# A hybrid HGRN2 and retention layer: rotation tables requested one product earlier, gate weights loaded four side steps ahead of their use

## The chip, the cores and the metric

The kernel runs on one NeuronCore of a Trainium2 chip. The metric is the device time of one execution in microseconds (us), the median of several executions. The engines are called as in the profile: PE (TensorE, matmuls), DVE (VectorE), ACT (ScalarE), POOL (GpSimd) and SP (SyncE, which here only issues DMAs). Each engine runs its own queue in order; DMAs are issued from the queues of SP, ACT and POOL.

## What is computed

The layer has one batch, 2048 positions and width 1024, all in float32. In the reference's own lines, cut to what matters here:

```
h = rms_norm(x, norm_g) * (1.0 + scale) + shift     # shift, scale, gate = silu(c) @ w_ada + b_ada
hq, hf, hi, hz, rq, rk, rv, rz, ga, gb = split(h @ w_in)
uA = head_rms_norm(hgrn2(hq, hf, hi), hg_norm_g) * silu(hz)
uB = head_rms_norm(retention(rotary(rq), rotary(rk), rv), ret_norm_g) * silu(rz)
x = x + gate * ((sigmoid(ga) * uA + sigmoid(gb) * uB) @ w_out)
out = rms_norm(x, final_g)
rotary: t1 * cos - t2 * sin, t1 * sin + t2 * cos    # the two halves of a head, by position
```

Two small pieces of it are touched by the change: the cosine and sine tables of the rotation, and the row `gate`, a product of silu(c) with a third of w_ada.

## The kernel before

**Halves and quads.** The positions are worked on in two halves of 1024. Each half runs the same list of 36 "quads" (ORDER, line 44): `a` makes query and forget gate of an HGRN2 head, `v` the values of one HGRN2 and one retention head, `b` query and key of a pair of retention heads, `A` and `B` the output gates of a head. So `b2` is the third retention pair; around it stand `v4 b2 a4 A2 B2 v5 a5 A3 B3 v6 b3 a6`.

**Products.** A quad is 256 columns of the projection for 1024 positions, made by seven products (a Strassen-like scheme, numbered 1 to 7, `product_order`, line 55). A product is 12 matmuls of 128x128 by 128x512, since each float32 operand is split into two fp32r parts. The products of neighbouring quads interleave: for quad n and the quad i ahead of it the order is (2,n), (7,i), (1,n), (5,n), (4,i), (3,n), (6,n). After products 1, 6, 7 and 4 of a quad, one quarter of its result is handed on (`deliver`): product 1 gives columns 0 of position block 0, 6 columns 1 of block 0, 7 columns 1 of block 1, 4 columns 0 of block 1.

**Background.** Beside the products runs other work, written as Python generators: `lanes` (HGRN2 outputs), `rets` (retention), `trees` (the decay tree of an HGRN2 head), and `side`, the work of the change. `bg.tick` is called four times in a product; each fourth tick advances `side` by one `yield`, so a `yield` stands for one product. `posts` are DMA stores that wait a number of ticks.

**Who orders the queues.** PE's instructions are kept in the order of the program. For the other engines the compiler places instructions by priority, which is the order of the program unless a block raises it, and by when their inputs and their buffer are expected to be ready. On the chip a queue then waits in order.

**Shared buffers.** Short-lived tiles of 512 columns come from one pool with six buffers, tag "tp" (`tmp`, NTP = 6): transposed values `vt`, sigmoids `sg` and `sz`, the tables `ct` and `sn`, the swapped half `sw` of the rotation, and the tiles of the side work. A tile that gets a buffer waits for the last reader of the tile before it, a DMA store included. Tag "mu" has four buffers, for the head outputs `mu` that are fetched back for the gating and for the accumulator `acc` of the side work. The PSUM tag "lv" has one bank: the levels of the trees use it, and the small matmuls of the side work too.

**Rotation tables** (`load_rot`, line 685). For each b quad and each of its two position blocks of 512, POOL issues one DMA of 256 KB for the cosines (`ct`, line 689) and two of 128 KB for the signed sines (`sn`, line 691). `take_b` (line 696) reads them: lines 702 and 703 make `sw`, 704 and 705 the result, on DVE, after products 1 and 6 with block 0's tables, after 7 and 4 with block 1's. The calls stand in the main loop: block 0 before product 2 of the b quad, block 1 before its product 6.

**Gate weights** (`ada_row`, line 1334). `gate` is made in two rows of 512 columns. For each of 8 tiles of weights (256 KB) SP issues a load `wg` (line 1338), and DVE adds the tile, scaled, to `acc` (lines 1342, 1344). After the eighth a bias `bg` is loaded, five steps pass, a matmul with a matrix of ones broadcasts the row over the partitions, DVE adds the bias (line 1351), and the row is stored. The rows start in the second half at product 1 of quad v4, one behind the other. Their result is read at the last quad (`load_wo`). In the first half other side work, `next_h` (line 1105), which prepares the second half's inputs, runs from v4 on and holds "tp" buffers too.

**POOL's other work** is small: the reciprocal root of the head norms (lines 186 to 189), on whose result ACT's scaling (line 897) waits, and which is queued with the table loads.

Of the kernel before, what the change touches and what calls it, by code (L numbers as in the profile page):

```python
# [46 lines left out]
def all_quads():  # L47
    return [(sb, x[0], int(x[1])) for sb in range(NSB) for x in ORDER.split()]


QUADS = all_quads()
NQ = len(QUADS)
# [11 lines left out]
def tile_hybrid(ctx: ExitStack, tc: tile.TileContext, a: dict, out: bass.AP):  # L64
# [35 lines left out]
    def bank(name, tag):  # L100
        return pp.tile([P, 512], F32, name=name, tag=tag, bufs=small[tag])

    def tmp(name, cols=512):
        return upool.tile([P, cols], F32, name=name, tag="tp", bufs=NTP)
# [466 lines left out]
    def product(i):  # L571
        m, q = seq[i]
        if m == 2:
            ps = yb[q] = bank(f"y{q}", xtag(q))
        elif m == 1:
            ps = xb[q] = bank(f"x{q}", xtag(q))
        elif m == 5:
            ps = vb[q] = bank(f"v{q}", "v")
        elif m == 3:
            ps = vb[q]  # L580
        else:
            ps = xb[q]
        W.pump(i + NBW)
        for j in range(4):
            if m == 6 and j == 2 and QUADS[q][1] in "AB":
                turned_u(QUADS[q][2], "AB".index(QUADS[q][1]), 0, "v")
            product_step(ps, m, q, j, m in (1, 2, 5) and j == 0, j == 3)
            bg.tick(1.0)
        W.parts.pop((m, q))
        after(m, q)  # L590
# [94 lines left out]
    def load_rot(q, tb):  # L685
        b = QUADS[q][0] * NBLK + tb
        ct, sn = tmp(f"ct{q}_{tb}"), tmp(f"sn{q}_{tb}")
        sl = slice(b * BLK, (b + 1) * BLK)
        G.dma_start(out=ct, in_=lin[0, :, sl].unsqueeze(0).broadcast_to([4, 32, BLK]))
        for two in range(2):  # L690
            G.dma_start(
                out=sn[64 * two : 64 * two + 64, :], in_=lin[1 + two, :, sl].unsqueeze(0).broadcast_to([2, 32, BLK])
            )
        rots[tb] = ct, sn
# [22 lines left out]
    def fetch_u(q, tb):  # L717
        sb, kind, h = QUADS[q]
        s, b = "AB".index(kind), sb * NBLK + tb
        n = 0  # L720
        while usent.get((s, h, b), bg.now) > bg.now - 5.0:
            bg.force()
            n += 1
            if n > 400:
                raise RuntimeError(f"no u {s} {h} {b}")
        if n:
            print("forced u", s, h, b, n)
        ut = mus[h, s, tb] = upool.tile([P, 512], F32, name=f"mu{s}_{h}_{b}", tag="mu", bufs=4)
        nc.sync.dma_start(out=ut, in_=ud[s, h, b])
# [443 lines left out]
    def change_h(sb):  # L1173
        for nm in ("A12", "S1", "A11", "S4", "S2", "S3", "A22"):
            for j in range(4):
                t = combos[sb, nm, j] = a_tile(f"{nm}_{sb}_{j}")
                nc.sync.dma_start(out=t[1].bitcast(F32), in_=hsd[sb, nm, j])
                split_here(t)
                yield
# [154 lines left out]
    def ada_row(j):  # L1334
        acc = upool.tile([P, 512], F32, name=f"acc{j}", tag="mu", bufs=4)
        for kt in range(KT):
            w = tmp(f"wg{j}_{kt}")
            nc.sync.dma_start(out=w, in_=a["w_gate"][j, kt])
            yield
            yield  # L1340
            if kt == 0:
                V.tensor_scalar(out=acc, in0=w, scalar1=sc[:, 0:1], scalar2=None, op0=ALU.mult)
            else:
                V.scalar_tensor_tensor(out=acc, in0=w, scalar=sc[:, kt : kt + 1], in1=acc, op0=ALU.mult, op1=ALU.add)
        bgt = tmp(f"bg{j}")
        nc.sync.dma_start(out=bgt, in_=a["bgate"][:, j * 512 : (j + 1) * 512].broadcast_to([P, 512]))
        for _ in range(5):
            yield
        ps = bank(f"gps{j}", "lv")
        PE.matmul(out=ps, lhsT=ones, rhs=acc, start=True, stop=True)  # L1350
        V.tensor_tensor(out=acc, in0=ps, in1=bgt, op=ALU.add)
        nc.sync.dma_start(out=gated[j], in_=acc)

    def load_wo():
        take("f", 1)
        both = upool.tile([P, 1024], F32, name="gates", tag="f", bufs=1)
        for nh in range(2):
            gate[nh] = both[:, nh * 512 : (nh + 1) * 512]
            nc.sync.dma_start(out=gate[nh], in_=gated[nh])
            for kt in range(KT):  # L1360
                t = wod[kt, nh] = a_tile(f"wo{kt}_{nh}")
                w = tmp(f"wr{kt}_{nh}")
                nc.sync.dma_start(out=w, in_=a["w_o"][kt // 2, nh][:, kt % 2, :])
                V.tensor_tensor(out=w, in0=w, in1=gate[nh], op=ALU.mult)
                split_into(t, w)
                yield

    def out_m(t):
        mts[t] = []
        for q4 in range(2):  # L1370
            m = a_tile(f"m{t}_{q4}")
            nc.sync.dma_start(
                out=m[1].bitcast(F32).rearrange("p (k t) -> p k t", t=P),
                in_=mT_dram[t // 4][4 * q4 : 4 * q4 + 4, :, (t % 4) * P : (t % 4 + 1) * P].rearrange("k p t -> p k t"),
            )
            split_here(m)
            mts[t].append(m)
# [42 lines left out]
    def meet_last():  # L1420
        tag, h, s, tb, fn = waits.pop(0)
        turned_u(h, s, tb, tag)
        fn()

    def some(gen, n):
        for _ in range(n):
            next(gen, None)
# [3 lines left out]
    for i in range(2, len(seq)):  # L1431
        m, q = seq[i]
        kind = QUADS[q][1]
        if m == 6 and 0 in waits:
            meet_last()
        if kind in "AB" and m in (2, 1):
            fetch_u(q, 2 - m)
        if kind == "b" and m == 2:
            load_rot(q, 0)
        if m == 2:  # L1440
            bg.gap = GAP_OF.get(QUADS[q][1:], bg.gap)
        if kind == "b" and m == 6:
            load_rot(q, 1)
        if QUADS[q] == (0, "v", 4) and m == 1:
            bg.side.append(next_h(1))
        if QUADS[q] == (1, "v", 4) and m == 1:
            bg.side.append(chain(ada_row(0), ada_row(1)))
        if (m, q) == (1, mid):
            pro["h"] = change_h(1)
        if (m, q - mid) in NEXT:  # L1450
            some(pro["h"], NEXT[m, q - mid])
        if q == NQ - 1:
            if m == 1:
                pro["w"] = load_wo()
            if m in (6, 7):
                out_m(m - 6)
            if m in (1, 3, 6, 7):
                some(pro["w"], 4)
            if m == 4:
                pro["fg"] = apool.tile([P, 1024], F32, name="fg", tag="A", bufs=NA)  # L1460
                nc.sync.dma_start(out=pro["fg"], in_=a["fg"].broadcast_to([P, 1024]))
                V.tensor_scalar(
                    out=pro["fg"], in0=pro["fg"], scalar1=float(D) ** 0.5, scalar2=None, op0=ALU.mult
                )
        product(i)
# [114 lines left out]
```

## Time and profile before

| | us |
|---|---|
| median of 3 runs | 2015.28 (2014.65 to 2016.09) |
| the profiled execution, its time | 2013.95 |
| its span, first to last instruction | 2012.2 |
| PE busy in the span | 1929.4 (96%) |
| DVE busy | 1419.7 (71%) |
| ACT busy | 984.5 (49%) |
| POOL busy | 300.6 (15%) |
| mean granted clock of PE | 0.988 |

A timeline row gives start, duration, engine (a "q" behind it: its queue issues a DMA), line, operation, output<-inputs, shapes and count; in brackets stands how long the engine was idle before, and what ended that. A waits row gives engine and line, what it waited for, total us, times, longest. In a windows row follow the stretch, its length, and for PE, PEld (weight loads), DVE, ACT and POOL the busy us and number of instructions, then the granted clock, the DMA share and GB/s. A chain row gives start, us and what the chain passed through.

### The profile page before, as it was taken

Reading aid. Unit: us, or ns where it says so; the run is one execution under the profiler, and the core shown is the slowest. Engines: PE = TensorE matmul, PEld = TensorE weight load, DVE = VectorE, ACT = ScalarE, POOL = GpSimd, SP = SyncE. Lnnn points to the kernel's source line nnn. Section 1 sums busy time; section 2 is a strip of 40 time slices with the busy share of each in tenths; the row PEclk is TensorE's granted clock in tenths of the full one; section 3 lists DMA queues with packets and bytes.
Section 4 is the critical chain, followed back from the end, with each engine's and each line's share of the span. In section 5 each row is a group of like instructions: output and inputs, shape, how many; then the busy total and the mean of one; then the engine's idle time right before and its main releaser. Section 6 shows DMA issues by size and latency. Waiting matters only on the chain.

```text
span 2012.2 us, 40017 instructions
## 1 busy us (share of the span) xinstructions
PE 1929.4 (96%) x15172; PEld 1581.1 (79%) x15172; DVE 1419.7 (71%) x2677; ACT 984.5 (49%) x2426; POOL 300.6 (15%) x522
## 2 busy tenths in 40 slices
PE   4899899998999999999999999999999999999998
PEld 3678688887788878887787788878788888887887
DVE  5896767676767777778977676777767775878332
ACT  4635444554456446546444545544454446454331
POOL 3102110221013211201003110211021102010000
PEclk7999999999999999999999999999999999999999
DMA  9345424354354554546545433454435433336442
GB/s 301 72 98 141 126 70 115 100 134 121 110 163 121 133 159 147 169 149 212 135 115 134 114 89 93 120 142 142 112 99 131 116 79 116 91 115 200 151 146 84
DMA packets 453121, 259.97 MB, mean 129 GB/s; under 512 B 171712, under 2 KB 406208, under 8 KB 452928
## 3 DMA queue, kind: packets, MB, share of 16 engines
q1 hardware_dynamic: 286752, 172.89, 30.3%
q10 hardware_dynamic: 153120, 76.04, 13.4%
q0 software_dynamic: 13056, 8.47, 1.7%
q8 instruction: 120, 1.97, 0.4%
q14 instruction: 73, 0.60, 0.1%
HBM read 188.03 MB, written 69.21 MB: 128 GB/s over the span
## 4 chain that ended last, share of the span: by engine, by line
PE 80%; DVE 6%; DMA 6%; ACT 2%; issue 2%; POOL 1%; SPq 1%; ACTq 0%; POOLq 0%; DVEq 0%
PE x L77 32%; PE v L77 17%; PE ops L77 9%; PE y L77 8%; PE E L77 4%; PE lv L77 3%; PE R L77 3%; PE uT L80 1%; DVE b L343 1%; DVE w L471 1%; DMA ud<-ur 1%; PE F L77 1%; DMA vd<-vt 1%; DMA wg<-in_w_gate_dram 1%; DMA sn<-lin 1%
## 5 line engine op out<-in xcount | busy, mean ns | idle before, releaser
L343 DVE TENSOR_TENSOR b<-w,b 128x512 fp32r<-128x512 f32 (+1 forms) x553 | 346.3, 634 | 223.0 <-ACT b L342 218.7
L342 ACT ACTIVATE b<-w 128x512 fp32r<-128x512 f32 (+1 forms) x553 | 316.7, 583 | 298.4 <-PE x L77 248.7
L77 PE MATMUL x<-S,b 128*128 128x512 f32 x1704 | 432.0, 398 | 4.4 <-DVE c L557 4.4
L77 PE MATMUL v<-S,b 128*128 128x512 f32 x1704 | 424.0, 397 | 4.2 <-ACT c L537 3.0
L77 PE MATMUL x<-A,b 128*128 128x512 f32 x1704 | 422.6, 395 | 0.9 <-DVE c L561 0.9
L77 PEld LDWEIGHTS v<-S,b 128*128 128x128 f32 x1704 | 316.9, 189 | 73.2 <-ACT c L537 4.1
L77 PEld LDWEIGHTS x<-A,b 128*128 128x128 f32 x1704 | 316.4, 189 | 67.9 <-issue 1.4
L77 PEld LDWEIGHTS x<-S,b 128*128 128x128 f32 x1704 | 311.7, 189 | 67.5 <-ACT uh L892 2.8
L77 PE MATMUL y<-A,b 128*128 128x512 f32 x840 | 207.2, 395 | 1.8 <-DVE q L644 1.4
L186 POOL TENSOR_SCALAR ssh<-ssh 128x1 f32<-128x1 f32 x128 | 51.3, 401 | 997.8 <-ACT uh L892 997.6
L471 DVE TENSOR_TENSOR w<-w,w 128x512 f32<-128x512 f32 x284 | 195.1, 687 | 3.4
L77 PEld LDWEIGHTS y<-A,b 128*128 128x128 f32 x840 | 155.0, 188 | 35.6 <-DVE q L644 1.8
L77 PE MATMUL ops<-wo,m 128*128 128x512 f32 x768 | 174.5, 389 | 0.0
L77 PEld LDWEIGHTS ops<-wo,m 128*128 128x128 f32 x768 | 144.1, 188 | 29.9
L537 ACT ACTIVATE c<-v 128x512 f32<-128x512 f32 x142 | 84.8, 597 | 162.5 <-PE v L77 150.5
L189 POOL TENSOR_TENSOR rrh<-ssh,mhalf 128x1 f32<-128x1 f32 x128 | 98.0, 766 | 10.6
L77 PEld LDWEIGHTS lv<-q,k 128*32 128x32 f32 (+1 forms) x5888 | 69.9, 109 | 36.5 <-issue 28.3
L557 DVE TENSOR_TENSOR c<-c,x 128x512 f32<-128x512 f32 x71 | 48.7, 686 | 66.0 <-PE x L77 65.8
L897 ACT ACTIVATE uh<-E,rrh 128x128 f32<-128x128 f32 x128 | 47.1, 368 | 93.3 <-POOL rrh L189 73.9
L77 PE MATMUL lv<-q,k 128*32 128x16 f32 (+2 forms) x5888 | 81.1, 187 | 10.6 <-DVE k L865 4.4
L864 DVE TENSOR_TENSOR q<-q,f 128x512 f32<-128x512 f32 x112 | 77.7, 694 | 7.9 <-PE lv L77 7.5
L537 ACT ACTIVATE c<-y 128x512 f32<-128x512 f32 x70 | 41.8, 598 | 79.4 <-PE y L77 79.3
(191 smaller groups left out, 2436.2 us busy)
## 6 DMA issues: line engine op xcount, KB each, us to landing
w<-in_w_d_dram ACTq DMA_DIRECT2D x128, 256.0 KB
w<-in_w_c_dram ACTq DMA_DIRECT2D x66, 256.0 KB
mu<-ud SPq DMA_DIRECT2D x64, 256.0 KB
w<-in_w_a_dram ACTq DMA_DIRECT2D x60, 256.0 KB
wa<-in_w_ada_dram SPq DMA_DIRECT2D x16, 512.0 KB
w<-in_w_b_dram ACTq DMA_DIRECT2D x32, 256.0 KB
vd<-vt SPq DMA_DIRECT2D x128, 64.0 KB
vh<-vd SPq DMA_DIRECT2D x64, 128.0 KB
```

The source lines that it names most:

```text
L77: return self.kept(nc.tensor.matmul(**kw))
L80: return self.kept(nc.tensor.transpose(**kw))
L186: G.tensor_scalar(out=ss, in0=ss, scalar1=n * EPS, scalar2=None, op0=ALU.add)
L189: G.tensor_tensor(out=dst, in0=ss, in1=mhalf.broadcast_to([P, w]), op=ALU.pow)
L342: parted["hi"] = S.activation(out=t[0], in_=src, func=AF.Copy)
L343: parted["lo"] = V.tensor_tensor(out=t[1], in0=src, in1=t[0], op=ALU.subtract)
L471: ins = V.tensor_tensor(out=out, in0=x, in1=y, op=ALU.add)
L537: S.activation(out=t, in_=ps, func=AF.Copy)
L557: V.tensor_tensor(out=t, in0=t, in1=xb[q], op=ALU.subtract)
L864: V.tensor_tensor(out=qv, in0=qv, in1=tv[:, :, :, 0:1].broadcast_to([P, NU, nb, m]), op=ALU.mult)
L897: behind(S.activation(out=dsts[i], in_=pos[i], func=AF.Copy, scale=rr[:, i : i + 1]), PE.last)
```

## The change

The load of the tables of block 0 of a b quad is called before product 6 of the quad ahead of it, not before product 2 of the b quad itself; in the regular order these are neighbours, so the call comes one product earlier. Block 1's call stays. In the very first b quad, b0 of the first half, product 2 runs ahead of its place, so there the call comes three products later. In `ada_row` four yields stand between the load of a tile and its use where two stood.

```
             nc.sync.dma_start(out=w, in_=a["w_gate"][j, kt])
-            yield
-            yield
+            for _ in range(4):
+                yield
             if kt == 0:
...
-        if kind == "b" and m == 2:
-            load_rot(q, 0)
+        if m == 6 and q + 1 < NQ and QUADS[q + 1][1] == "b":
+            load_rot(q + 1, 0)
         if m == 2:
```

## Prediction

> **What bounds the kernel now.** I read the page first (spans, chain), then the waits of PE and VectorE, then the timelines around each wait, last the windows for the granted clock.
>
> ```profile
> span 2012.2 us, 40017 instructions
> PE 1929.4 (96%) x15172; PEld 1581.1 (79%) x15172; DVE 1419.7 (71%) x2677; ACT 984.5 (49%) x2426; POOL 300.6 (15%) x522
> DVE sw L702 <- DMA sn<-lin: 7.9, 2, 4.1
> DVE acc L1344 <- DMA wg<-in_w_gate_dram: 7.6, 4, 4.3
> ```
>
> TensorE (PE) is busy 96% and sets the end; only its idle time, 2012.2 - 1929.4 = 82.8 us with start and tail, can be won. What the change aims at are two waits of VectorE (DVE): 7.9 us for sine tables, 7.6 us for gate weights. DVE is busy 71%, so such a wait counts only where PE then stands.
>
> ```profile
> 1333.26 0.61 SPq L1338 DMA_DIRECT2D wg<-in_w_gate_dram  x1
> 1333.97 5.95 SPq L656 DMA_DIRECT2D vd<-vt  x4
> 1333.26 9.11 DMA wg<-in_w_gate_dram
> 1342.46 0.75 DVE L1344 SCALAR_TENSOR_TENSOR acc<-wg,sc,acc 128x512 f32<-128x512 f32 x1 [4.28 <-DMA wg<-in_w_gate_dram]
> 1343.85 0.69 DVE L702 TENSOR_TENSOR sw<-c,sn 64x512 f32<-64x512 f32 x1
> 1354.01 0.80 PE L77 MATMUL R<-vh,k 128*128 128x128 f32 x2 [4.68 <-DVE st L975]
> 1350.00:1355.00 5.00, 0.99 (x4) 0.99 (x5) 4.91 (x9) 2.61 (x6) 0.00 (x0) 0.64 0.30 89
> 1355.00:1360.00 5.00, 5.00 (x19) 4.07 (x18) 2.14 (x5) 2.23 (x7) 1.32 (x2) 0.68 0.60 184
> ```
>
> This is the largest PE gap after the start, in quad b2 of the second half. A gate tile is asked of SP at 1333.26 and lands 9.11 us later; DVE reaches its use 4.92 us after the asking (1342.46 - 4.28 - 1333.26) and stands 4.28 us. The work behind it keeps DVE full, the state update L975 comes late, PE stands 4.68 us. Then the granted clock (the eighth number of a window: 0.64, 0.68) costs 0.99 x 0.36 + 5.00 x 0.32 = 1.96 us more. Loss 6.64 us.
>
> ```profile
> 1402.62 0.75 DVE L1344 SCALAR_TENSOR_TENSOR acc<-wg,sc,acc 128x512 f32<-128x512 f32 x1 [1.56 <-DMA wg<-in_w_gate_dram]
> 1423.40 0.69 PE L77 MATMUL lv<-q,k 128*16 128x16 f32 x64 [2.01 <-DVE k L868]
> 465.53 1.42 POOL L691 DMA_DIRECT2D sn<-lin  x2 [3.18 <-DMA vd<-vt]
> 471.63 0.69 DVE L702 TENSOR_TENSOR sw<-c,sn 64x512 f32<-64x512 f32 x1 [4.08 <-DMA sn<-lin]
> 474.79 0.49 PE L77 MATMUL R<-vh,k 128*128 128x128 f32 x2 [1.67 <-DVE st L975]
> 478.94 2.99 PE L77 MATMUL y<-A,b 128*128 128x512 f32 x12 [0.46 <-DVE ro L704]
> 485.28 2.99 PE L77 MATMUL x<-S,b 128*128 128x512 f32 x12 [2.68 <-DVE c L557]
> 706.14 0.49 PE L77 MATMUL R<-vh,k 128*128 128x128 f32 x2 [1.63 <-DVE st L975]
> ```
>
> A second gate wait (1.56 us) lies in a stretch of full DVE before a PE gap of 2.01 us. The sine wait of the first half's b2 (4.08 us) is followed by PE gaps of 1.67 + 0.46 + 2.68 = 4.81 us. The other sine wait, in that half's b3, is followed by 1.63.
>
> **The change part by part.** *Tables.* load_rot issues three DMAs on GpSimd (POOL), one ct and two sn.
>
> ```profile
> 431.57 0.80 POOL L689 DMA_DIRECT2D ct<-lin  x1
> 432.36 1.33 POOL L691 DMA_DIRECT2D sn<-lin  x2
> 450.44 0.68 DVE L702 TENSOR_TENSOR sw<-c,sn 64x512 f32<-64x512 f32 x1
> 1056.85 1.31 POOL L691 DMA_DIRECT2D sn<-lin  x2 [0.57 <-DVE b L343]
> 1066.59 0.68 DVE L702 TENSOR_TENSOR sw<-c,sn 64x512 f32<-64x512 f32 x1
> DMA to landing us min/median/max: 5.3/7.7/9.7
> ```
>
> Only the call for block 0 moves, from before product 2 of a b quad to before product 6 of the quad ahead. Block 0's tables are not late: in the first half's b2 they are asked at 432.36 and used at 450.44, 18.08 us later; the tightest pair has 1066.59 - 1056.85 = 9.74 us, and landing takes at most 9.7. The late tables (465.53, used 471.63) are block 1's, asked in load_rot(q, 1), which stays. They were late because POOL waited for a buffer that a store of vt still held. So the gain here is nothing. The cost: the three issues, 0.80 + 1.33 = 2.13 us, pass one product's rstd operations on POOL, and ScalarE's scalings wait for those; and two of the six "tp" buffers are held one product longer, so the transposed value tile of that product takes a later one. Bounds 0 to 2.13; a gain below nothing I exclude, since no block 0 table is waited for. Value 0: nearest to the slack of 18.08. (In the first half's b0 the call comes three products later instead; POOL does nothing else between in the trace.)
>
> *Gate weights.* The side work steps once per product; the code now puts four products between load and use, not two. The same 16 loads and 16 DVE operations stay, so work adds nothing.
>
> ```profile
> 1336.98 2.99 PE L77 MATMUL y<-A,b 128*128 128x512 f32 x12
> 1315.89 2.88 PE L77 MATMUL y<-A,b 128*128 128x512 f32 x12
> ```
>
> These are product 2 of two neighbouring quads: 21.09 us for seven, 3.01 each. Two more give a lead of 4.92 + 6.02 = 10.94 us, over 9.11: the use at 1342.46 no longer waits. But what is late next? Two DVE operations behind, at 1343.85, comes the sw of the second product, which needs a "tp" buffer. The latest store of vt left SP until 1333.97 + 5.95 = 1339.92, and
>
> ```profile
> 685.03 5.29 DMA vd<-vt
> 456.33 8.57 DMA vd<-vt
> ```
>
> say that such a store lands 5.29 to 8.57 us later, 1345.2 at the earliest. If sw has that buffer, the stall moves behind the acc and shrinks by 1343.85 - 1342.46 = 1.39 us only, the gap by as much, to 3.29.
>
> ```profile
> 485.00:490.00 5.00, 4.72 (x21) 3.95 (x22) 3.42 (x8) 2.79 (x7) 2.67 (x6) 1.00 0.46 138
> 505.02 1.12 PE L80 MATMUL uT<-ident,mu 128*128 128x128 f32 x4 [2.91 <-ACT c L537]
> 505.00:510.00 5.00, 4.98 (x21) 4.29 (x22) 2.24 (x5) 2.46 (x7) 1.70 (x4) 0.67 0.40 114
> ```
>
> A gap of 2.68 left the clock at 1.00, one of 2.91 brought 0.67, so at 3.29 the clock's 1.96 would stay lost. If sw has another buffer, the whole 4.28 goes, the gap falls to 0.40 and the 1.96 return: 6.24. Bounds 1.39 to 6.24. I take the upper: sw ran at 1343.85, before such a store can have landed, so it had another buffer in this execution. Term **-6.24**.
>
> The Trainium skill (DMA: Bandwidth & Descriptors, "Anatomy of one DMA — SWDGE (gpsimd) path") fits a DMA's time as 2.0 us plus bytes / 436e3, by estimate 2.6 us for these 256 KB; then a lead of 4.92 us is enough already, and this term would be 0. The 9.11 row speaks against it.
>
> Second gate wait: 1.56 us goes, from a gap of 2.01. Bounds 0 to 2.01; **-1.56**, the wait itself.
>
> What the stretching adds: the rows now run through 2 x (8 x 4 + 5) = 74 steps, not 2 x (8 x 2 + 5) = 42, so to the second half's b3, which had no such company. First, a gate or bias tile holds a buffer there as the x tiles did in the first half.
>
> ```profile
> 1558.08 8.26 SPq L656 DMA_DIRECT2D vd<-vt  x4
> 1564.07 0.68 DVE L702 TENSOR_TENSOR sw<-c,sn 64x512 f32<-64x512 f32 x1
> 442.64 0.69 PE L77 MATMUL lv<-q,k 128*64 128x64 f32 x16 [0.89 <-ACT rb L1128]
> SPq L729 <- DVE mu L775: 18.4, 1, 18.4
> ```
>
> The vt store there left SP until 1566.34, behind the sw at 1564.07. Bounds 0 to 4.81 (the first half's b2); **+1.63**, the row of its b3. Second, the first row's broadcast matmul falls 16 products later, between two levels of a tree that share its one PSUM bank; a like matmul left a gap of 0.89. Bounds 0 to 0.89, **+0.89**. Third, acc keeps one of four "mu" buffers through A3 and B3; in A2 and B2 SP stood 18.4 us for such a buffer in the stretch from 1385 to 1430, and the PE gap of 1423.40 was DVE's, not a load's. 0, up to that 2.01.
>
> Sum: -6.24 - 1.56 + 1.63 + 0.89 = -5.28 us on the profiled execution (2013.95, of which 1.75 outside the span): 2008.67. The median, 2015.28, is 1.33 above it: 2010.0. A difference under 0.2% (4.03 us), about what a measurement of this kernel can tell, counts as no change.
>
> **The rivals.** *All of it is won*: b3 has room and the broadcast's bank is free in time. -6.24 - 2.01 = -8.25, so 2007.0. For it: both are measured stalls. Against it: 1558.08's row and the 0.89.
>
> *Slower: the buffer shortage moves.* In the second half's b2 only 1.39 is won, since sw now gets the vt store's buffer; in b3, newly full, the tables or sw wait as in the first half's b2: 4.81, and after a gap above 2.9 the clock's 1.96, together 6.77; the bank 0.89; the second wait's 1.56 still goes. -1.39 - 1.56 + 6.77 + 0.89 = +4.71: 2020.0. It makes the kernel slower once b3 loses over 6.1 us. For it: the order of requests for "tp" changes in every b quad, so the lucky buffer of 1343.85 is not sure. Against: the bias tile is freed just ahead of b3's second sw.
>
> *The steps do not do what they say*: the order in the queues is made by readiness too.
>
> ```profile
> 1385.69 0.75 DVE L1344 SCALAR_TENSOR_TENSOR acc<-wg,sc,acc 128x512 f32<-128x512 f32 x1 [0.72 <-DMA wg<-in_w_gate_dram]
> 1398.64 2.88 PE L77 MATMUL v<-S,b 128*128 128x512 f32 x12
> ```
>
> This acc, the fourth of the second row, stands in the code behind the product at 1398.64, and ran 13 us ahead of it, waiting for its load. If all move up so, as many waits remain: 2015.3, give or take 2. Against it: in b2, where DVE is full, the lead was near its two products, 4.92 of 6.02. By the fit of the Trainium skill (DMA: Bandwidth & Descriptors, same section) this would be the time as well.
>
> **How the numbers follow.** The forecast 0.42, all won 0.12, shortage 0.22, steps without effect 0.24. The bounds of the forecast's terms reach to within 4.03, for which I give 0.10 of its 0.42. Faster 0.32 + 0.12 = 0.44; slower 0.22; within 0.2% 0.24 + 0.10 = 0.34. Range 2006.5 to 2019.5: from under the first rival to just short of the second, which leaves out half of its 0.22 and some 0.06 below. The forecast's own range is 2007.0 to 2015.0.
>
> **What would show it.** Right: no DVE wait for wg above 1 us; PE gap before the R matmul of b2 under 1 us, clock 1.00 after it; the two sine waits of the first half still there. Wrong: a DVE wait at L702 of 4 us in the second half's b2 or b3 on sn or vd; a PE gap behind the broadcast matmul above 1 us; sine waits gone in the first half, which I hold to be block 1's; the gate's loads still only two products ahead of their use.

## The result, and the profile after

The changed kernel takes 2028.6 us (2026.65 to 2028.72), the kernel before 2015.05 beside it (2014.65 to 2016.09): a ratio of 1.0070, 95% interval 1.0053 to 1.0087, or 13.6 us more. The forecast was 2010.0, the upper end of its range 2019.5. One more execution of the changed kernel took 3834.4 us and is left out of these times. The profiled execution took 2028.72, its span 2027.0.

From the page and the waits of the changed kernel:

```profile
PE 1940.5 (96%) x15172; PEld 1588.1 (78%) x15172; DVE 1419.2 (70%) x2677; ACT 983.4 (49%) x2426; POOL 298.8 (15%) x522
DVE acc L1344 <- DMA wg<-in_w_gate_dram: 15.2, 5, 6.9
DVE sw L702 <- DMA sn<-lin: 7.4, 2, 4.0
ACT f L636 <- DMA rqk<-rd: 4.5, 1, 4.5
```

The gate waits that the steps were to remove have doubled, from 7.6 to 15.2 us. The two sine waits are as long as before (7.9 us there). A wait of ScalarE for `rqk`, a read of the stored tensor `rd`, which its operation at L636 doesn't use, has grown from 1.3 to 4.5 us.

PE runs the same 15172 matmuls in nearly the same order, so the start of one and the same matmul in both traces tells where time was lost ("us of starts" below is a change of this difference):

| matmul, start before | start after | difference |
|---|---|---|
| 160.00 | 159.26 | -0.74 |
| 172.01 | 176.22 | +4.21 |
| 1039.99 | 1046.24 | +6.25 |
| 1279.31 | 1287.98 | +8.67 |
| 1345.03 | 1353.68 | +8.65 |
| 1362.00 | 1363.68 | +1.68 |
| 1394.27 | 1405.05 | +10.78 |
| 1428.00 | 1437.85 | +9.85 |
| 1439.90 | 1454.57 | +14.66 |
| 1899.94 | 1914.71 | +14.77 |

Single executions of one kernel differ by several us (before: 2007.75 to 2022.73 over all runs below), in part by small gaps and clock drops that come and go, so such a table tells places; the sizes are taken from the ratios of the experiments. Four places stand out.

**b1 of the first half (about 165 us), +5.** First the kernel before, timeline, one row of its chain and one window; then the same of the changed one:

```profile
151.01 2.87 SPq L1013 DMA_DIRECT2D rqk<-rd  x2
161.00 0.81 ACT L636 ACTIVATE f<-sg,lb,omlb 128x512 f32<-128x512 f32 x1 [1.34 <-DMA rqk<-rd]
163.05 2.99 PE L77 MATMUL v<-S,b 128*128 128x512 f32 x12 [0.64 <-ACT c L537]
167.44 0.78 POOL L689 DMA_DIRECT2D ct<-lin  x1
151.01 9.22 DMA rqk<-rd
165.00:170.00 5.00, 5.00 (x27) 4.24 (x26) 1.94 (x5) 2.83 (x8) 2.90 (x5) 1.00 0.63 128
```

```profile
150.31 2.86 SPq L1013 DMA_DIRECT2D rqk<-rd  x2
154.24 0.68 POOL L689 DMA_DIRECT2D ct<-lin  x1 [34.61 <-DMA rqk<-rd]
162.92 0.61 ACTq L456 DMA_DIRECT2D w<-in_w_b_dram  x1
163.57 0.81 ACT L636 ACTIVATE f<-sg,lb,omlb 128x512 f32<-128x512 f32 x1 [4.46 <-DMA rqk<-rd]
165.62 2.58 PE L77 MATMUL v<-S,b 128*128 128x512 f32 x7 [3.95 <-ACT c L537]
150.31 12.53 DMA rqk<-rd
165.00:170.00 5.00, 4.38 (x12) 3.47 (x13) 2.25 (x5) 2.56 (x8) 0.75 (x2) 0.66 0.76 158
```

The cos table is asked for at 154.24, not 167.44. The read rqk, asked for at 150.31, lands 12.53 us later, at 162.84; in the kernel before it took 9.22 us. What waits for it is no computation but a weight load in ScalarE's queue (L456, 162.92), and behind that load stand f and then c (L537), on which PE waits 3.95 us, after which the granted clock is 0.66. Here f starts 0.73 us behind the landing; where no chain row is shown below, the read's time is worked out with that.

The trace also keeps the signals by which each transfer reports its landing, sixteen for this read, one for each part. Before, fourteen had come 4.86 us after the asking and the last two at 9.21 and 9.22; in the changed kernel fourteen at 4.89 and the last two at 9.26 and 12.53. The two stores of rd just ahead of the read land in two late parts only, 9.5 to 10.2 us after their asking in both kernels. The early cos table has twelve signals within 3.36 us and four late ones, the last at 8.84. So the delay lies in two parts of the read, and it is likely that they stand behind the late parts of the stores and of the table; no run tried that by itself.

**b2 of the second half, -7 and then +9.**

```profile
1361.64 1.41 SPq L1013 DMA_DIRECT2D rqk<-rd  x3
1363.15 0.41 SPq L1338 DMA_DIRECT2D wg<-in_w_gate_dram  x1
1366.03 0.75 DVE L1344 SCALAR_TENSOR_TENSOR acc<-wg,sc,acc 128x512 f32<-128x512 f32 x1 [6.89 <-DMA wg<-in_w_gate_dram]
1367.44 4.13 PE L77 MATMUL x<-S,b 128*128 128x512 f32 x10 [2.24 <-DVE b L343]
1371.83 0.60 SPq L1338 DMA_DIRECT2D wg<-in_w_gate_dram  x1
1381.63 0.75 DVE L1344 SCALAR_TENSOR_TENSOR acc<-wg,sc,acc 128x512 f32<-128x512 f32 x1 [5.75 <-DMA wg<-in_w_gate_dram]
1383.30 0.49 PE L77 MATMUL R<-vh,k 128*128 128x128 f32 x2 [2.82 <-DVE st L975]
```

The gap of 4.68 at the R matmul is gone, and with it 7 us (+8.65 to +1.68). But VectorE reached the fifth tile's use at 1366.03 - 6.89 = 1359.14, four microseconds ahead of the asking at 1363.15, which stood on SP behind the three rqk reads. The sixth tile waits 5.75 us more. Two PE gaps follow, of 2.24 and 2.82. The sixth tile's load shows the late parts again: fourteen of its sixteen signals had come 3.87 us after the asking, the last two at 9.14 and 9.78, and two stores of rd were asked for just ahead of it (1370.74 and 1371.29).

**The broadcast (about 1440 us), +4.8.**

```profile
1439.44 1.02 PE L77 MATMUL gps<-acc,ones 128*128 128x512 f32 x2
1442.08 0.68 DVE L1351 TENSOR_TENSOR acc<-gps,bg 128x512 f32<-128x512 f32 x1
1442.82 0.87 PE L77 MATMUL lv<-q,k 128*32 128x32 f32 x32 [2.35 <-DVE acc L1351]
```

Row 0's broadcast matmul lies between two levels of a tree, as the prediction said; the next level waits 2.35 us until VectorE has emptied the bank. Some 0.9 us of the 4.8 is the broadcast matmul itself, which ran at 1374.51 before and so is missing from the 9 us above.

**Between 172 and 1280 us, +4**, in steps of 1 to 2 us that come and go from run to run; the experiments below don't confirm a cause there.

### The profile page after: what moved, and what is told of

It reads as the page before. It is cut to its first block, busy times and chain, and to the rows that moved or that the text cites. A ratio compares the mean times of both kernels' runs of the same rounds, so it can differ in the third digit from the quotient of the medians.

```text
span 2027.0 us, 40019 instructions
## 1 busy us (share of the span) xinstructions
PE 1940.5 (96%) x15172; PEld 1588.1 (78%) x15172; DVE 1419.2 (70%) x2677; ACT 983.4 (49%) x2426; POOL 298.8 (15%) x522
## 4 chain that ended last, share of the span: by engine, by line
PE 82%; DMA 6%; DVE 5%; ACT 2%; issue 2%; POOL 1%; SPq 1%; ACTq 0%; POOLq 0%; DVEq 0%
PE x L77 33%; PE v L77 17%; PE ops L77 9%; PE y L77 8%; PE E L77 4%; PE lv L77 3%; PE R L77 3%; PE uT L80 1%; DMA rd<-c 1%; DMA w<-in_w_a_dram 1%; DVE b L343 1%; DMA ud<-ur 1%; PE F L77 1%; DVE w L471 1%; DMA wg<-in_w_gate_dram 1%
## 5 line engine op out<-in xcount | busy, mean ns | idle before, releaser
L77 PE MATMUL v<-S,b 128*128 128x512 f32 x1704 | 430.0, 401 | 6.6 <-ACT c L537 5.4
L77 PEld LDWEIGHTS v<-S,b 128*128 128x128 f32 x1704 | 321.1, 192 | 77.3 <-ACT c L537 7.0
L537 ACT ACTIVATE c<-v 128x512 f32<-128x512 f32 x142 | 84.6, 596 | 163.4 <-PE v L77 148.1
L537 ACT ACTIVATE c<-y 128x512 f32<-128x512 f32 x70 | 41.8, 596 | 80.1 <-PE y L77 79.9
```

What stands on the lines that cost most here:

```text
L77: return self.kept(nc.tensor.matmul(**kw))
L537: S.activation(out=t, in_=ps, func=AF.Copy)
```

## The experiments

Theory T1: the table move and the steps each lose, at the places above. Rivals: one of the two carries all (T2 the steps, T3 the tables). Ratios are to the kernel before on the same chip, with 95% intervals; 0.1% is 2.0 us.

**1. The table move alone.**

```
-        if kind == "b" and m == 2:
-            load_rot(q, 0)
+        if m == 6 and q + 1 < NQ and QUADS[q + 1][1] == "b":
+            load_rot(q + 1, 0)
```

> Only the call for block 0's tables is moved; the gate rows keep their two products. Theory (T1): two separate losses, one from each part; the starts of the same matmuls are 8.2 us later by 1280 us, before any side work differs, so this kernel takes 6 to 10 us more than the one before, with a PE gap of some 4 us ahead of a v product near 165 us and a granted clock below 0.75 behind it. Rival T2: the table move is harmless by itself, as the prediction had it, and the offsets before 1280 us are chance of one profiled execution: within 2 us of before. Rival T3: the table move carries all of the loss: 12 to 15 us more.

Ratio 1.0041 (1.0026 to 1.0057): 8.3 us more, with a PE gap of 4.16 at 166.1. Its gate waits sum to 14.0 us, though the steps are before's two. T1 holds; "the table move is harmless" (T2) falls, and so does T3, whose 12 us lie above the interval's 11.5.

**2. The four steps alone.**

```
-            yield
-            yield
+            for _ in range(4):
+                yield
```

> Only the four steps; the tables are asked for where they were. T1: the start differences behind 1280 us sum to +6.6 us (-6.0 in the second half's b2, -1.0 at the second gate wait, +8.5 from gate waits that come later in b2, A3 and B3, +4.3 behind the broadcast matmul), so 4 to 9 us more than before, with DVE waits for gate tiles of more than 10 us in sum. T2 (the steps carry all of the loss): 12 to 15 us more. T3 (all of the loss is the table move's): within 2 us or faster.

Ratio 1.0017 (1.0004 to 1.0031): 3.4 us more, a little under T1's 4 to 9. Gate waits 14.4 us in 5; no gap over 1.1 at 165. T2's 12 to 15 us fall here too. T3's "within 2 us" isn't excluded by this interval (0.8 to 6.2 us); experiment 1 excludes it. 8.3 + 3.4 = 11.7 lies in the whole change's interval (10.7 to 17.5 us).

**3. Four steps, gate operations held.**

```
             for _ in range(4): yield
...
+                ins = V.scalar_tensor_tensor(out=acc, in0=w, ...)
+            behind(ins, PE.last)
```

> The four steps, and each gate operation of VectorE held in the order behind the last product issued ahead of it, so that it cannot move up before its fourth product. T1 (the use is placed by expected readiness and not by the steps, so the lead did not grow where it was needed): DVE waits for gate tiles fall under 2 us in sum, the 8.5 us of later gate waits goes, and the time is 1 to 5 us below before's (-7 from the two old waits, +4.3 from the broadcast matmul that stays). Rival (loads are asked for too late on SP, behind waiting transfers, whatever the place of the use): waits for gate tiles of 6 us or more stay and the time is within 2 us of the kernel with the steps alone.

Ratio 0.9990 (0.9980 to 1.0001), 2.0 us less: inside T1's 1 to 5, though the interval just includes no change at all. No gate operation waits for its tile any more, so the rival falls:

```profile
1365.18 0.84 SPq L1338 DMA_DIRECT2D wg<-in_w_gate_dram  x1
1379.60 0.74 DVE L1344 SCALAR_TENSOR_TENSOR acc<-wg,sc,acc 128x512 f32<-128x512 f32 x1
1418.65 0.69 PE L77 MATMUL lv<-q,k 128*16 128x16 f32 x64 [2.00 <-DVE k L868]
```

14.42 us between the sixth tile's asking and its use; over the 16 tiles 10.3 to 38.5 us, where the changed kernel has 2.9 to 15.7, its waits included, and the kernel before 2.7 to 15.8. What stays is the broadcast: the tree's level waits 2.35 us for the bank again. The third row is the place of before's second gate wait; it comes up again in the account below.

**4. Two steps, held.** Experiment 3's `behind`, with before's two yields.

> The kernel before, two steps, with each gate operation held behind the last product issued ahead of it. T1: the uses in the second row, which ran up to four products early, now stand at their two products, the first row's little moved; the 4.28 us wait at b2 stays since its lead was near two products already, and the time is within 3 us of before. Rival (holding is itself the whole gain, the number of steps is not): gate waits under 1 us in sum and 4 us or more below before.

Ratio 1.0003 (0.9993 to 1.0012). Two waits of 3.3 us each remain at b2, where two products are too few. T1 holds: by the waits it takes the steps and the holding together. By time alone experiments 3 and 4 hardly part, since their intervals overlap.

**5. The table move only at the first half's b1.**

```
+        if kind == "b" and m == 2 and QUADS[q] != (0, "b", 1):
             load_rot(q, 0)
+        if m == 6 and q + 1 < NQ and QUADS[q + 1] == (0, "b", 1):
+            load_rot(q + 1, 0)
```

> The kernel before, with block 0's tables asked for one product sooner only for the first half's quad b1. The engines' orders differ from before's in two places: on GpSimd the three table DMAs pass one head's two rstd operations, on ScalarE one scaling moves by two places. T1 (of the 8.3 us that the table move costs alone, 3 to 5 arise here, from the table transfers that now run beside the rd stores, the rqk reads and the vdr stores): 3 to 5 us more than before, a PE gap of about 4 us ahead of a v product near 165 us. Rival (the loss is spread over all b quads): within 1.5 us of before, and no such gap.

Ratio 1.0014 (1.0005 to 1.0023): 2.8 us, just under T1's 3 to 5. The rival's 1.5 us lie inside the interval too, but its "no such gap" does not hold:

```profile
150.98 2.92 SPq L1013 DMA_DIRECT2D rqk<-rd  x2
154.97 0.69 POOL L689 DMA_DIRECT2D ct<-lin  x1 [35.59 <-DMA rqk<-rd]
163.82 0.81 ACT L636 ACTIVATE f<-sg,lb,omlb 128x512 f32<-128x512 f32 x1 [4.63 <-DMA rqk<-rd]
165.87 4.59 PE L77 MATMUL v<-S,b 128*128 128x512 f32 x12 [4.42 <-ACT c L537]
```

The changed kernel's picture, from this one call: rqk takes 163.82 - 0.73 - 150.98 = 12.1 us. In this one profile 5.4 us of starts are lost there, more than the ratio says.

**6. The table move everywhere but there.** The two conditions of 5 turned round.

> The kernel before, with block 0's tables asked for sooner in all b quads but the first half's b1. Here the orders differ on GpSimd in one place (two rstd operations of one head, passed by the tables), and on VectorE and SyncE around the gate operations of the second half's b2. T1: what is left of the 8.3 us, 3 to 5 us more than before, out of gate waits in the second half's b2 that sum to 12 us or more where before had 7.6. Rival (all of the table move's loss is in b1): within 1.5 us of before.

Ratio 1.0020 (1.0007 to 1.0034): 4.0 us, as T1 has it; the rival's 1.5 us lie at the interval's lower end. Gate waits 13.5 us in 6:

```profile
1339.87 0.59 SPq L1338 DMA_DIRECT2D wg<-in_w_gate_dram  x1
1349.34 0.75 DVE L1344 SCALAR_TENSOR_TENSOR acc<-wg,sc,acc 128x512 f32<-128x512 f32 x1 [6.93 <-DMA wg<-in_w_gate_dram]
1350.84 4.58 PE L77 MATMUL x<-S,b 128*128 128x512 f32 x12 [4.26 <-DVE c L557]
1388.02 0.75 DVE L1344 SCALAR_TENSOR_TENSOR acc<-wg,sc,acc 128x512 f32<-128x512 f32 x1 [1.01 <-DMA wg<-in_w_gate_dram]
1394.94 0.66 PE L80 MATMUL uT<-ident,mu 128*128 128x128 f32 x4 [2.17 <-ACT c L537]
```

The load lands as late as before's (9.47 us), but VectorE is at its use 2.54 us behind the asking, before 4.92; a later tile waits 3.24 more. The table move, two yields untouched, has shifted the gate operations in VectorE's order. The gap of 4.26 only takes the place of before's 4.68 at 1354.01. What is new is the gap of 2.17 at 1394.94, behind another gate wait and with a granted clock of 0.66 after it: 4.3 us of starts (+5.77 to +10.05).

**7. The whole change, gate operations held.**

> The whole change, tables and four steps, with the gate operations held behind their products. T1 (the table move costs in two places, the transfers at b1 and the order of gate operations in the second half's b2, and holding takes away the second): 2 to 4 us more than the four steps held without the table move, so a ratio to before of 1.000 to 1.001, PE gap of 4 us near 165 us still there, gate waits under 2 us in sum. Rival (the table move's loss in the second half has nothing to do with the gate operations): 6 us or more above the held steps, ratio over 1.002.

Ratio 1.0011 (0.9997 to 1.0025), just above T1's 1.000 to 1.001; the rival's "over 1.002" isn't excluded by the interval. The gap at b1 is there, smaller than expected (2.47 at 166.78), and no gate operation waits for its tile. So the waits, more than the time, say that the second half's share of the table move was the order of the gate operations, and that b1's is its own.

**8. Held, both broadcasts five products later.** `range(5)` becomes `range(10)` ahead of `gps`.

> The four steps with the gate operations held behind their products, and the broadcast matmul of each row five products later than in the kernel with held operations, out of the tree of quad B2. T1: the PE gap of 2.35 us on the lv bank near 1430 us and the lower clock behind it go, 3 to 4 us less than with held operations alone: 2008 to 2010, 4 to 6 us below before. Rival (the bank's wait is hidden or comes back behind the next tree's matmuls): the same gap at another tree, and a time within 1.5 us of the kernel with held operations.

Ratio 1.0010 (1.0000 to 1.0020): T1's time is missed by 6 us. The rival is right that the time comes back, but not where: the gap at 1430 did go, and a new one came, not at a tree:

```profile
1577.51 1.01 SPq L710 DMA_DIRECT2D rd<-c  x2
1583.10 0.61 ACTq L456 DMA_DIRECT2D w<-in_w_d_dram  x1
1583.81 0.63 ACT L342 ACTIVATE b<-w 128x512 fp32r<-128x512 f32 x1 [8.58 <-DMA rd<-c]
1585.47 0.49 PE L77 MATMUL R<-vh,k 128*128 128x128 f32 x2 [2.54 <-DVE st L975]
```

Again a weight load in ScalarE's queue stands for a transfer that has nothing to do with it, here the store of rd at 1577.51; ScalarE idles 8.58 us, PE 2.54, and with the lower clock behind it 7.5 us of starts go (-6.99 to +0.51). In the kernel with held operations the load at this place waits for no such transfer. Which of its forerunners a load waits for has changed with the order of the transfers. The traces show the link: all transfers of SP and ScalarE report their landing on the same eight semaphores, this load on the one (108) that the store at 1577.51 uses, and the queue waits for 108 just before the load; at b1 the load and the read share 107. No run gave a load a semaphore of its own.

**9. Held, row 0's broadcast five products later, row 1's where it was.** Row 1's loads have three steps, not four, which makes up for the delay.

```
+            for _ in range(4 - j): yield
...
+        for _ in range(10 - 2 * j): yield
```

> Four steps for row 0, three for row 1, gate operations held behind their products, row 0's broadcast matmul five products later than with held operations (behind the tree of 1390 to 1437 us), row 1's where it was. T1 (the row 0 broadcast costs 3.3 us in the tree's bank, and what undid that gain with both broadcasts late was a weight load of ScalarE at 1583 us that stood 8.58 us for a store of rd): no lv gap above 1.2 us near 1430, no gap above 1.2 us near 1585, 3 to 4 us less than with held operations alone: ratio to before 0.9965 to 0.9980, faster than both kernels. Rival (such waits turn up somewhere whenever the order of transfers changes): a new PE gap of over 2 us behind 1430 us and a ratio above 0.9985.

Ratio 0.9959 (0.9941 to 0.9977): 8 us less than before, faster than both kernels, more than T1's 0.9965 to 0.9980.

```profile
1427.94 0.70 PE L77 MATMUL lv<-q,k 128*32 128x32 f32 x32
1434.70 0.69 PE L77 MATMUL lv<-q,k 128*64 128x64 f32 x16
1443.61 1.02 PE L77 MATMUL gps<-acc,ones 128*128 128x512 f32 x2
```

The broadcast lies behind the tree, and no level waits. Between the matmuls that start at 1428.00 and 1439.90 in before, the kernel with held operations loses 3.3 us (-4.75 to -1.47), 0.9 of it the broadcast matmul itself, and this one nothing (-1.74 at both). The 6 us between the ratios of 3 and 9 are more than that; the rest isn't traced to a place, and row 1's three steps may have a part in it.

**10 to 15. What in the table move delays the read at b1.** Six kernels, each the one before with one thing added, or that of experiment 5 with one thing taken away.

*10: a spare copy of 256 KB of rd to DRAM on POOL's queue.*

```
+            if (s, p, b) == (1, 0, 1):
+                G.dma_start(out=spare, in_=rd[0, 0][1][:, 512:1024])
```

> The kernel before, and one more transfer that nothing needs: GpSimd's queue copies 256 KB of rd to a spare tile in DRAM, as many rows of as many bytes as one cos table, at the time (about 154 us) at which the moved cos table is asked for. No buffer changes hands, and the orders of all engines stay. T1 (the loss at b1 is the collision of transfers): the rqk read asked for at 151 us lands 1.5 to 3 us later than before's 160.2, the PE gap near 165 us grows to 2 to 4 us, and the time to 2 to 5 us above before. Rival (the loss comes from the rstd operations that the tables pass, or from buffers taken sooner, and not from traffic): rqk lands as before, gap under 1.2 us, time within 1.5 us of before.

Ratio 1.0005 (0.9993 to 1.0018); rqk 163.71 - 0.73 - 153.60 = 9.4 us, PE gap 0.16. My theory in this form, that any 256 KB beside the read do it, falls.

```profile
153.60 2.92 SPq L1016 DMA_DIRECT2D rqk<-rd  x2
156.32 0.55 POOL L713 DMA_DIRECT2D spare<-rd  x1 [34.30 <-DMA rd<-c]
163.71 0.82 ACT L637 ACTIVATE f<-sg,lb,omlb 128x512 f32<-128x512 f32 x1 [1.90 <-DMA rqk<-rd]
```

*11: the copy in 512 pieces of 512 bytes.*

```
+                G.dma_start(out=spare[:, 0:P].rearrange("(c p) e -> p c e", p=P),
+                            in_=rd[0, 0][1][:, 512:1024].rearrange("p (c e) -> p c e", e=P))
```

> As the kernel with the spare copy of 256 KB on GpSimd's queue, but the copy is cut into 512 pieces of 512 bytes; in the earlier copy the 256 KB showed as 80 packets, where the moved tables show 709. Orders and buffers are before's again. T1 in a narrower form (the collision is one of packets, not of bytes): the rqk read takes 11 to 13 us from issue to landing, not 9.3, ScalarE stands over 3.5 us at the f of L636, the PE gap near 165 us is 2 to 4.5 us, and the time 2 to 4 us above before. Rival (it is not traffic but the table loads themselves, their buffers or the rstd operations that they pass): rqk 9 to 10 us, gap under 1.2 us, time within 1.5 us of before.

Ratio 0.9998 (0.9982 to 1.0014), rqk 9.4 us. Inconclusive: the copy shows as 80 packets again, so the pieces were not made smaller.

*12: the buffers claimed sooner, the transfers in the old place.* `load_rot` split into the two `tmp` calls, early, and the three DMAs, late.

> The first half's b1 again: the two buffers of block 0's tables are claimed one product sooner, but their three transfers stay where they were in GpSimd's queue. The orders of all engines are those of the kernel before. Theory Q (what costs at b1 is the tables' own transfers running beside the rqk read): rqk takes 8.6 to 9.7 us, as in every kernel so far with late tables (nine of them, 8.66 to 9.63), the gap near 165 us is under 1.7 us, and the time within 1.5 us of before. Rival B (what costs is that two of the six tp buffers are claimed sooner, so that others wait): rqk 11.8 to 12.6 us, gap 2.4 to 4.4, 2 to 4 us above before.

Ratio 1.0000 (0.9988 to 1.0013). It is the transfers and not the buffers:

```profile
149.83 3.14 SPq L1018 DMA_DIRECT2D rqk<-rd  x2
160.17 0.81 ACT L636 ACTIVATE f<-sg,lb,omlb 128x512 f32<-128x512 f32 x1 [2.15 <-DMA rqk<-rd]
166.61 0.78 POOL L694 DMA_DIRECT2D ct<-lin  x1
```

The read takes 9.6 us, and PE has no gap there.

*13: a quarter of each table sooner.* The same split, with columns 0 to 127 fetched early.

> The first half's b1: the buffers are claimed sooner and a quarter of each table (128 of 512 columns) is fetched sooner, in three transfers as in the change; the other three quarters are fetched in the old place. Theory Q by bytes (a quarter of the traffic, a quarter of the harm): rqk 9.2 to 10.5 us, gap under 2 us. Theory Q by pieces (as many rows, as many transfers: the harm comes from their number, whatever their length): rqk 11.5 to 12.6 us, gap 2.4 to 4.4. Rival B: as by pieces, so this run tells something only beside the run with the buffers alone.

rqk takes 160.95 - 0.73 - 149.99 = 10.2 us and PE has no gap over 0.1 us there, as "by bytes" has it. Yet the ratio is 1.0060 (1.0037 to 1.0083); the profile shows no loss at b1, but one of 3.3 us of starts between 1345 and 1362, with a gate wait of 6.84 us at 1347.96. Why three more transfers between 154 and 168 us should do that is open.

*14: the copy in the cos table's form, 32 rows read four times.*

```
+                G.dma_start(out=spare.rearrange("(f p) t -> f p t", f=4),
+                            in_=rd[0, 0][1][0:32, 512:1024].unsqueeze(0).broadcast_to([4, 32, 512]))
```

> The kernel before with the spare copy again, but in the cos table's form: 32 rows of rd read four times over, as a block of 4 x 32 rows, into the spare 256 KB in DRAM, at the time at which the first copy ran. Theory F (the form counts: a transfer whose slowest dimension is 4 loads few of the queues that the rqk read needs): rqk 11.5 to 12.6 us from issue to landing, gap near 165 us over 2 us. Theory D (the form does not count; what harms is writing to SBUF beside the read, or the two sine transfers behind the cos table): rqk 9.0 to 9.7 us, gap under 1.7 us. The Trainium skill (DMA: Bandwidth & Descriptors, "Why a DMA increments its semaphore by 16 and not by 1") says that a transfer is spread over as many engines, up to 16, as divide the slowest dimension of both sides, which would be 4 for the cos table, 2 for each sine load and 16 for the first copy; no trace here shows single engines.

Ratio 1.0038 (1.0017 to 1.0060), rqk 163.94 - 0.73 - 150.72 = 12.5 us:

```profile
150.20 0.69 POOL L713 DMA_DIRECT2D spare<-rd  x1 [30.13 <-DMA rd<-c]
150.72 2.91 SPq L1019 DMA_DIRECT2D rqk<-rd  x2
163.94 0.81 ACT L637 ACTIVATE f<-sg,lb,omlb 128x512 f32<-128x512 f32 x1 [1.16 <-DMA rqk<-rd]
165.99 4.60 PE L77 MATMUL v<-S,b 128*128 128x512 f32 x12 [2.52 <-ACT c L537]
```

As many bytes to the same place, in the other form, bring the delay. Two things are not alike: the rows copied, and the time, since this copy was asked for 0.5 us ahead of the read and the first 2.7 us behind it. (The changed kernel's cos table was asked for 3.9 us behind it.)

*15: the early tables as eight transfers of 32 rows without repetition.*

```
+            for i in range(4):
+                G.dma_start(out=ct[32 * i : 32 * i + 32, :], in_=lin[0, :, sl])
+            for i in range(4):
+                G.dma_start(out=sn[32 * i : 32 * i + 32, :], in_=lin[1 + i // 2, :, sl])
```

> Block 0's tables asked for sooner at the first half's b1, each as four transfers of 32 rows without repetition, in place of one with 4 x 32 and two with 2 x 32 rows: eight issues on GpSimd, the same bytes. Theory F: each of them spreads, rqk takes 9 to 10.5 us, the gap falls from 4.4 to under 2 us and the time to within 1.5 us of before, or below. Theory D (the bytes into SBUF count, whatever their form): rqk 11.5 to 12.6 us, gap 2.4 to 4.5 us, 2 to 4 us above before.

```profile
150.77 2.92 SPq L1020 DMA_DIRECT2D rqk<-rd  x2
154.78 1.51 POOL L691 DMA_DIRECT2D ct<-lin  x3 [35.55 <-DMA rqk<-rd]
160.79 0.82 ACT L636 ACTIVATE f<-sg,lb,omlb 128x512 f32<-128x512 f32 x1 [1.81 <-DMA rqk<-rd]
```

Three of the eight run at the early place, the read takes 9.3 us and PE has no gap there: for the form (F). But the ratio is 1.0040 (1.0026 to 1.0053), so the time that b1 gives back is lost elsewhere, as in 13; F's time is missed. In its profile 6.2 us of starts go between 172 and 500 us and 3.4 between 1040 and 1150, from causes not traced. The other five issues come behind 166 us, so the test is not of all bytes.

Over all kernels the read at b1 takes 8.7 to 9.7 us wherever neither tables nor the copy in their form run beside it, 11.9 to 12.6 with the tables early as the change has them. In every one of them fourteen of its sixteen parts have landed within 5.0 us, so only the last two parts differ. That the form counts is likely from 10, 14 and 15 and from these signals, not settled.

## Why the prediction was wrong

**Tables, value 0, bounds 0 to 2.13: this step failed first.** That block 0's tables are not late was right, as was that the two sine waits stay (7.9 to 7.4 us). Wrong was the bound. It was made from POOL's issues (0.80 + 1.33) and from buffers, but a call that is moved takes its transfers with it, here to a place where the rqk read and the stores of rd and vdr ran, and the read's landing released ScalarE's queue. Measured alone: 2.8 us at b1. A second price was not seen at all: the move shifts the gate operations in the second half, 4.0 us. The whole move measures 8.3 us (5.2 to 11.5), which the two make up within their intervals. Why the read takes longer beside the tables is likely their form, and not settled.

**"Two more give a lead of 10.94", term -6.24.** The wait and the gap at that place went, about 7 us of starts. The step that failed is taking products in the code for time on the engines: the leads became 2.9 to 15.7 us and not 10.94, no longer on the whole than before's 2.7 to 15.8, of which the prediction took one place as the rule; and the waits came back at the next tiles, for 9.1 us of starts (+1.68 to +10.78). The row of the prediction's third rival (an operation 13 us ahead of its place in the code) said so; the rival had the mechanism and was priced at 2015.3, as if a moved wait cost the same. By the fit of the Trainium skill (DMA: Bandwidth & Descriptors, "Anatomy of one DMA — SWDGE (gpsimd) path"), which is stated for GpSimd's transfers, a load of 256 KB takes, by estimate, 2.6 us; of these loads, issued by SP, the trace agrees for one (asked at 1363.15, used 2.88 us later) and not for the next (9.80).

**Second gate wait, -1.56:** the gap of 2.01 became 1.05, but the wait was not its cause. In experiment 3, without any gate wait, the gap is 2.00 (the row at 1418.65). In the changed kernel no gate operation at all runs in the 36 us ahead of it; that this shortened it is argued, not tried.

**Buffers in the second half's b3, +1.63:** nothing. No sine or store wait came there, and no PE gap over 1 us. With it the rival "slower, the buffer shortage moves" falls, though its sign came true.

**Broadcast in the tree's bank, +0.89:** the place was right, the size was not: 2.35 us of gap. The bound came from an ACT read of the bank; here a matmul, its wait and VectorE's place for the add lie between.

**The sum** had its two largest costs, the tables and the gate waits that come back, at zero. The measured time lies beyond all of its rivals; the nearest, at 2020.0, is so by another mechanism.

## What to carry to other kernels

A load that is asked for sooner also moves its traffic: look at what lands in that stretch, and at what its landing releases, before calling it free. Look also at the parts of a transfer that land last, and at what was asked for just ahead of it. A distance counted in program steps is a lead only if the use is held to its step; so held, with the broadcast out of the tree, four and three steps give 0.4% where four alone cost 0.2%. Where queues are refilled by a scheduler, a change in one place reorders another, so each part is to be timed alone and the traces laid side by side.

## What the runs showed of the hardware

- A weight load in ScalarE's queue can stand for a landing that it doesn't need, and stop the arithmetic behind it: 4.46 us at b1, 8.58 us in experiment 8. In both traces the load reports on the same semaphore as the landing that it waits for (107 and 108), one of eight that SP's and ScalarE's transfers share.
- The same 256 KB gate load took at most 2.88 us (1363.15) or 9.80 (1371.83), 9 us apart. Fourteen of the sixteen parts landed within 2.71 and 3.87 us; of the second load the last two came at 9.14 and 9.78, behind two stores of rd that land in two late parts each (6.57 to 9.65 us).
- The granted clock was 0.66 after a PE gap of 2.17 us (experiment 6), while a gap of 2.68 in the prediction's rows left it at 1.00. Gaps of 2 to 3 us may cost the clock or not.
- Of two copies of 256 KB by POOL's queue, the one of 128 plain rows left the rqk read at 9.4 us, the one of 32 rows read four times made it 12.5. The Trainium skill (DMA: Bandwidth & Descriptors, "Why a DMA increments its semaphore by 16 and not by 1") says that a transfer is spread over the largest number of engines, up to 16, that divides the slowest dimension of both sides, 16 for the one and 4 for the other. That agrees with the two times and with the landing signals: the last two of the first copy came 5.23 and 5.50 us after its asking and the others within 3.28; the last four of the second came at 4.87, 4.87, 9.22 and 9.98 and the others within 2.25. Which engines carried them no run here shows.
